# First feed-forward matrix by seven block products instead of eight

## The chip, the cores and the metric

The kernel runs on one core of a Trainium2 chip, as one launch. The metric is device time in microseconds, the median of several runs. TensorE multiplies matrices into PSUM banks, VectorE (DVE) and ScalarE (ACT) do elementwise work and read PSUM, GpSimd (POOL) does elementwise work in SBUF, and the DMA queues move data; SyncE's queue (SP) issues the loads of weights.

## The reference

One inference step of a two-layer encoder over 512 prompt positions and 32 positions of a later chunk, 544 columns together, in float32. Each of the two layers is

```
x = LN_0(alpha*x + 0.5*SwiGLU_1(x))           # d = 1024, hidden 2816
proj = x @ w_in                               # pooling, short convolution, q, k, v
x = LN_1(alpha*x + concat(pool, conv, attn) @ w_out)
x = LN_2(alpha*x + 0.5*SwiGLU_2(x))

def swiglu(x, w_in, w_out):
    gate, up = jnp.split(x @ w_in, 2, axis=-1)
    return (jax.nn.silu(gate) * up) @ w_out
```

so there are four feed-forward (SwiGLU) layers, each with a first matrix of 1024 x 5632 (gate and up) and a second of 2816 x 1024. The outputs are y, the new keys and values, and the states of pooling and convolution.

## The kernel before

Activations stand transposed: 8 tiles (k = 0 to 7) of 128 features by T = 544 columns, which are treated as two halves of HALF = 272 (`HS`), since a PSUM bank holds 512 floats. `y` is the residual in float32. The matmuls run on pairs of float32r tiles: `split` writes a rounded part (`hh`, by ScalarE) and the rest (`hl`, by VectorE). A product is three matmuls, high weights by high input and low weights by high input (`mm_h`, L199) and high weights by low input (`mm_l`, L204), summed in PSUM.

`Weights` streams the weights in the order of `specs`. `load` (L163) fetches one tile of 128 x 1024 (or 128 x 896) into a `raw` buffer, of which there are two, through SP's queue, and `group` splits it by 512 columns into `whi` (ScalarE, L159) and `wlo` (VectorE, L160); the ring has W_BUFS = 8 groups, and `get` keeps the loads two tiles ahead. All instructions pass through a framework that adds the semaphores and fixes, before the run, each engine's order of instructions; instructions written earlier have priority, but one whose buffer isn't free yet can be passed.

`ffn` goes over the 22 hidden tiles in three parts (FSPLIT = 8, 7, 7). A hidden tile is two weight tiles, gate and up: `mm2` runs 2 halves x 8 k x 3 matmuls for each; then ScalarE takes Silu of the gate (L448), VectorE multiplies by the up (L449), and `split` makes the pair `hx`. After each part the second matrix adds its contribution, 8 output tiles of 48 or 42 matmuls, into `y` (`resid`, L343 and L345). The last part is `out_phase`, which runs normalisation (`LN`) beside its last matmuls: sums of squares, `stats`, `spread`, then per k `centre` (L316) and `scale` (L322, L327, L332, and GpSimd's L333). The next stage's first two weight tiles are multiplied in `start`, half by half as the normalised tiles appear; their accumulators are handed on as `pre`. There are six PSUM banks in the pool `ps` and two in `po`.

Of the kernel before, what the change touches and what calls it, by code (L numbers as in the profile page):

```python
# [10 lines left out]
F32 = mybir.dt.float32  # L11
# [17 lines left out]
NF = D_FF // P  # L29
FSPLIT = (8, 7, 7)  # L30
NB = 2
W_BUFS = 8
RAW_BUFS = 2
# [15 lines left out]
UW = 640  # L49

# [17 lines left out]
def encoder_kernel(  # L68
# [28 lines left out]
    tp = ctx.enter_context(tc.tile_pool(name="tp", bufs=4))  # L97
# [46 lines left out]

    class Weights:


        def __init__(self, specs):
            self.specs, self.used, self.loaded, self.ready = specs, 0, 0, []

        def fetch(self):
            self.loaded += 1
            return wp.tile([P, NK * P], F32, tag="raw", name="raw", bufs=RAW_BUFS)

        def group(self, raw, g, n):
            e = min(G, n - g)
            hi = wp.tile([P, G], F32R, tag="whi", name="whi", bufs=W_BUFS)
            lo = wp.tile([P, G], F32R, tag="wlo", name="wlo", bufs=W_BUFS)
            S.activation(out=hi[:, :e], in_=raw[:, g:g + e], func=AF.Copy)  # L159
            V.tensor_tensor(out=lo[:, :e], in0=raw[:, g:g + e], in1=hi[:, :e].bitcast(F32), op=ALU.subtract)  # L160
            return hi, lo

        def load(self):  # L163
            src, n = self.specs[self.loaded]
            raw = self.fetch()
            nc.sync.dma_start(out=raw[:, :n], in_=src)
            self.ready.append([self.group(raw, g, n) for g in range(0, n, G)])

        def first(self, x):

            specs = self.specs[:2]
            raws = [self.fetch() for _ in specs]
            self.ready = [[], []]
            for i in range(NK // 4):
                ks, cs = slice(4 * i, 4 * i + 4), slice(i * G, (i + 1) * G)
                nc.sync.dma_start(out=ya[:, ks, HS[0]], in_=xT[:, ks, HS[0]])
                for (src, n), raw in zip(specs, raws):
                    nc.sync.dma_start(out=raw[:, cs], in_=src[:, cs])
                for k in range(NK)[ks]:
                    split(y[k], x[k], HS[0])  # L180
                for raw, out in zip(raws, self.ready):
                    out.append(self.group(raw, i * G, NK * P))
            nc.sync.dma_start(out=ya[:, :, HS[1]], in_=xT[:, :, HS[1]])

        def ahead(self, n):

            while self.loaded < min(self.used + n, len(self.specs)):
                self.load()

        def get(self, n=2):  # L190
            self.used += 1
            self.ahead(n)
            return self.ready.pop(0)

    def mm_h(acc, w, x, k, h, first):

        cs = slice((k % 4) * P, (k % 4) * P + P)
        for i, v in enumerate(w[k // 4]):
            PE.matmul(acc[:, :HALF], v[:, cs], x[k][0][:, HS[h]], start=first and i == 0, stop=False)  # L199

    def mm_l(acc, w, x, k, h, last):

        cs = slice((k % 4) * P, (k % 4) * P + P)
        PE.matmul(acc[:, :HALF], w[k // 4][0][:, cs], x[k][1][:, HS[h]], start=False, stop=last)  # L204
# [30 lines left out]

    class LN:
# [9 lines left out]
        def ln_tile(self, name):  # L246
            return tp.tile([P, T], F32, tag="ln", name=name, bufs=3)

        def half_tile(self, tag, name, bufs):
            return tp.tile([P, HALF], F32, tag=tag, name=name, bufs=bufs)  # L250
# [29 lines left out]
        def add_last(self, m, acc, h):  # L280
            c, q = y[m][:, HS[h]], self.half_tile("z", "sq", 4)
# [23 lines left out]
        def spread(self, h, psum):  # L305

            d = self.half_tile("dg", "diag", 2)[:CH].rearrange("p (c t) -> p c t", c=NCH)
# [10 lines left out]
        def scale(self, h, k):  # L318
            l, j, sl = self.l, self.j, HS[h]
            c = y[k][:, sl]  # L320
            z = self.half_tile("z", "z", 4)
# [25 lines left out]
    def out_phase(l, j, x, ks, alpha):  # L347
# [4 lines left out]
        first = NK - nb  # L352
        for m in range(first):
# [37 lines left out]
        if ln.final:  # L391
# [7 lines left out]
            mean = ln.half_tile("dg", "mean", 2)  # L399
# [13 lines left out]
    def start(x, step, hooks, done):  # L413

        ws = [W.get(0), W.get(0)]
        accs = [(bank(), bank()), (bank(), bank())]
        todo = [(h, k) for h in range(2) for k in range(NK)][done:]
        for h in range(2):
            for k in range(NK):
# [8 lines left out]
                if h == 1 and k in (3, 6):  # L428
                    W.ahead(k // 3)
# [4 lines left out]

    def ffn(l, f, x, pre):
        for s, n in enumerate(FSPLIT):
            hs = []
            for i in range(n):
                if pre:
                    ga, ua = pre  # L440
                    pre = None
# [542 lines left out]
```

## Time and profile before

| | us |
|---|---|
| median of 3 runs (lowest, highest) | 2107.07 (2106.86, 2107.29) |
| profiled execution, its own time | 2106.86 |
| its span, first to last instruction | 2104.7 |

| engine | busy us | share of the span | instructions |
|---|---|---|---|
| TensorE, matmuls | 2079.3 | 99% | 16286 |
| VectorE | 1013.1 | 48% | 1970 |
| ScalarE | 771.6 | 37% | 1591 |
| GpSimd | 228.8 | 11% | 216 |

The profile's page has the busy time of each engine, the span in 40 slices with a digit for the busy tenths, the chain of work that ended last followed back from the end, and the costliest groups of instructions: line, engine, operation, output and inputs, shape and count, then busy time and mean ns of one, then the engine's idle time just before them and what ended most of it. Matmuls are pipelined, so the time of one is longer than the distance from one to the next. The timeline merges neighbours of one kind into one row (x3 is three of them). HBM moved 179.88 MB in and 8.34 MB out.

### The profile page before, as it was taken

The numbers are of one execution on the slowest core, as the hardware profiler recorded it, in microseconds if no ns is written. First come the engines' busy times: TensorE is split into PE (matmuls) and PEld (weight loads), VectorE is DVE, ScalarE is ACT, GpSimd is POOL, SyncE is SP. The second block draws the span as 40 slices with busy tenths as digits, with TensorE's granted clock in tenths as the row PEclk, the third lists the DMA queues.
The fourth block names the chain that finished last, engine by engine and source line by source line (L and its number), as shares of the span: only waits on it lengthen the run. The fifth ranks groups of instructions, "written<-read, shape, count | busy, mean of one in ns | idle before, by whom it ended". The sixth has DMA issues, their size and how long they took to land.

```text
span 2104.7 us, 38545 instructions
## 1 busy us (share of the span) xinstructions
PE 2079.3 (99%) x16286; PEld 2042.2 (97%) x16286; DVE 1013.1 (48%) x1970; ACT 771.6 (37%) x1591; POOL 228.8 (11%) x216
## 2 busy tenths in 40 slices
PE   9999999999999999999999999999999999999997
PEld 9999999999999999999999999999999999999997
DVE  4333333776556333333653333347766553333337
ACT  5323223565435323223443232235653353222233
POOL 0000000511133000000420000006011320000003
PEclk9999999999999999999999999999999999999999
DMA  7322222132232222222232222222321222222221
GB/s 240 99 91 83 90 91 84 59 115 92 62 119 81 91 86 86 84 98 82 70 101 83 89 88 89 89 85 67 109 93 54 78 91 82 90 89 82 91 83 61
DMA packets 61749, 189.13 MB, mean 90 GB/s; under 512 B 8932, under 2 KB 13156, under 8 KB 61576
## 3 DMA queue, kind: packets, MB, share of 16 engines
q1 hardware_dynamic: 52592, 173.18, 25.9%
q10 hardware_dynamic: 8984, 13.49, 2.0%
q8 instruction: 128, 2.10, 0.4%
q14 instruction: 45, 0.37, 0.1%
HBM read 179.88 MB, written 8.34 MB: 89 GB/s over the span
## 4 chain that ended last, share of the span: by engine, by line
PE 95%; DVE 2%; POOL 1%; ACT 1%; issue 1%; DMA 0%; SPq 0%; POOLq 0%; ACTq 0%
PE b L199 59%; PE b L204 30%; PE b L629 1%; PE b L628 1%; PE o L644 1%; POOL xl L333 1%; PE b L609 0%; ACT ya L327 0%; DVE z L322 0%; PE b L716 0%; POOL rstd L302 0%; PE b L682 0%; DVE diag L308 0%; DVE acc L286 0%; PE b L311 0%
## 5 line engine op out<-in xcount | busy, mean ns | idle before, releaser
L199 PE MATMUL b<-xh,whi 128*128 128x272 f32 x3456 | 1000.0, 291 | 6.2 <-ACT xh L332 3.7
L199 PE MATMUL b<-xh,wlo 128*128 128x272 f32 x3456 | 993.5, 289 | 0.3 <-DVE wlo L160 0.3
L204 PE MATMUL b<-xl,whi 128*128 128x272 f32 x3456 | 978.2, 288 | 0.2
L160 DVE TENSOR_TENSOR wlo<-raw,whi 128x512 fp32r<-128x512 f32 (+1 forms) x656 | 469.7, 719 | 694.8 <-ACT whi L159 692.7
L159 ACT ACTIVATE whi<-raw 128x512 fp32r<-128x512 f32 (+1 forms) x656 | 403.3, 619 | 858.7 <-PE b L204 569.8
L199 PEld LDWEIGHTS b<-xh,whi 128*128 128x128 f32 x3456 | 651.7, 189 | 9.5 <-ACT xh L332 5.9
L199 PEld LDWEIGHTS b<-xh,wlo 128*128 128x128 f32 x3456 | 653.1, 189 | 1.5 <-DVE wlo L160 0.8
L204 PEld LDWEIGHTS b<-xl,whi 128*128 128x128 f32 x3456 | 644.6, 188 | 2.1 <-POOL xl L333 1.5
L199 PE MATMUL b<-hh,wlo 128*128 128x272 f32 x1408 | 406.2, 289 | 0.0
L199 PE MATMUL b<-hh,whi 128*128 128x272 f32 x1408 | 405.2, 288 | 0.0
L204 PE MATMUL b<-hl,whi 128*128 128x272 f32 x1408 | 404.6, 287 | 0.0
L199 PEld LDWEIGHTS b<-hh,wlo 128*128 128x128 f32 x1408 | 264.9, 188 | 0.2
L204 PEld LDWEIGHTS b<-hl,whi 128*128 128x128 f32 x1408 | 264.9, 188 | 0.2
L199 PEld LDWEIGHTS b<-hh,whi 128*128 128x128 f32 x1408 | 264.9, 188 | 0.0
L278 POOL TENSOR_TENSOR ya<-ya,shift 128x544 f32<-128x544 f32 x14 | 24.8, 1792 | 1412.9 <-DVE wlo L160 1386.4
L448 ACT ACTIVATE sg<-b 128x272 f32<-128x272 f32 x176 | 69.6, 397 | 213.1 <-PE b L204 213.0
L449 DVE SCALAR_TENSOR_TENSOR sg<-b,sg 128x272 f32<-128x272 f32 x176 | 77.6, 441 | 130.9 <-PE b L204 119.2
L343 DVE SCALAR_TENSOR_TENSOR ya<-ya,b 128x272 f32<-128x272 f32 x88 | 38.5, 438 | 88.7 <-PE b L204 87.8
L333 POOL TENSOR_TENSOR xl<-ya,xh 128x272 fp32r<-128x272 f32 x80 | 70.3, 901 | 30.8 <-ACT xh L332 25.1
L345 DVE TENSOR_TENSOR ya<-ya,b 128x272 f32<-128x272 f32 x108 | 46.7, 433 | 54.0 <-PE b L204 53.8
L232 ACT ACTIVATE hh<-sg 128x544 fp32r<-128x544 f32 (+1 forms) x100 | 59.1, 591 | 32.6 <-DVE sg L449 32.5
L233 DVE TENSOR_TENSOR hl<-sg,hh 128x544 fp32r<-128x544 f32 (+1 forms) x100 | 65.2, 652 | 7.2 <-ACT hh L232 7.1
(183 smaller groups left out, 1455.9 us busy)
## 6 DMA issues: line engine op xcount, KB each, us to landing
raw<-in_w SPq DMA_DIRECT2D x206, 512.0 KB, 3.5
raw<-in_w SPq DMA_DIRECT2D x64, 448.0 KB, 3.3
raw<-in_wi SPq DMA_DIRECT2D x40, 512.0 KB, 3.5
raw<-in_wo SPq DMA_DIRECT2D x16, 512.0 KB, 3.5
U<-scr ACTq DMA_DIRECT2D x8, 320.0 KB, 4.8
out_nkT<-k ACTq DMA_DIRECT2D x8, 272.0 KB, 2.1
out_nvT<-vT ACTq DMA_DIRECT2D x8, 272.0 KB, 2.1
out_yT<-ya SPq DMA_DIRECT2D x16, 136.0 KB, 1.8
```

What stands on the lines that cost most here:

```text
L159: S.activation(out=hi[:, :e], in_=raw[:, g:g + e], func=AF.Copy)
L160: V.tensor_tensor(out=lo[:, :e], in0=raw[:, g:g + e], in1=hi[:, :e].bitcast(F32), op=ALU.subtract)
L199: PE.matmul(acc[:, :HALF], v[:, cs], x[k][0][:, HS[h]], start=first and i == 0, stop=False)
L204: PE.matmul(acc[:, :HALF], w[k // 4][0][:, cs], x[k][1][:, HS[h]], start=False, stop=last)
L232: S.activation(out=hh[:, sl], in_=t[:, sl], func=AF.Copy)
L233: (eng or V).tensor_tensor(out=hl[:, sl], in0=t[:, sl], in1=hh[:, sl].bitcast(F32), op=ALU.subtract)
L278: POOL.tensor_tensor(out=c, in0=c, in1=self.s, op=ALU.subtract)
L333: POOL.tensor_tensor(out=xl[:, sl], in0=c, in1=xh[:, sl].bitcast(F32), op=ALU.subtract)
L343: V.scalar_tensor_tensor(out=c, in0=c, scalar=ALPHA, in1=a, op0=ALU.mult, op1=ALU.add)
L345: V.tensor_tensor(out=c, in0=c, in1=a, op=ALU.add)
L448: S.activation(out=sg[:, sl], in_=g[:, :HALF], func=AF.Silu)
L449: V.scalar_tensor_tensor(out=sg[:, sl], in0=u[:, :HALF], scalar=0.5, in1=sg[:, sl], op0=ALU.mult, op1=ALU.mult)
```

## The change

The first matrix of a hidden tile is a product of 2 x 2 blocks: rows gate and up (2 blocks of 128), the sum over k in two parts (k = 0 to 3 and 4 to 7), columns in two halves. Before, that is eight block products of four k each. Now 20 of the 22 hidden tiles of each feed-forward layer take seven (the Strassen-Winograd form), of sums of weight blocks with sums of input blocks; the first two (NPLAIN = 2) keep eight. The second matrix is unchanged.

- `Weights.sums`: a tile's four blocks of 128 x 512 (two fetches of 512 KB) give seven groups to be split instead of four, with four VectorE additions in float32. The ring is 10 groups instead of 8, `raw` 3 buffers instead of 2; loads run one such tile ahead (`get`).
- `Blocks`: once a feed-forward layer, for each of four pairs (k, k + 4) of the normalised input, four VectorE operations of 272 columns make the sums `s56` and `s73`, and two splits make the pairs that are multiplied.
- `seven`: the products, 12 matmuls each, into three banks in the order a, b, a, c, a, c, a. The products in a are summed up there, and so are those in c; after each product `after[i]` reads the bank (`hidden`): after 1, 3 and 4 a copy by ScalarE, after 2, 5, 6 and 7 an operation by VectorE. A product that adds to a bank must wait for the reading before it.
- `plan`: a part of the second matrix comes one hidden tile later than before, but for the last. The last hidden tile is split whole, not by halves.
- Memory: the normalisation's tiles and the block sums share a pool of XB = 18 tiles (`big`), whose place the mixer's tiles take in between, and `out_phase` of the mixer is called after the mixer's pool is closed. `tmp` has 5 buffers instead of 4.

```diff
 FSPLIT = (8, 7, 7)
+NPLAIN = 2
-W_BUFS = 8
-RAW_BUFS = 2
+W_BUFS = 10
+RAW_BUFS = 3
...
+XB = 18
...
+        def add(self, a, b):
+            r = big["pool"].tile([P, G], F32, tag="sum", name="sum", bufs=4)
+            V.tensor_tensor(out=r, in0=a, in1=b, op=ALU.add)
+            return r
+
+        def sums(self, src):
+            b11, b12, b22, b21 = self.blocks(src)
+            g11, g21 = self.group(b11), self.group(b21)
+            r1 = self.add(b11, b12)
+            r2 = self.add(r1, b22)
+            g2, g1 = self.group(r2), self.group(r1)
+            g3 = self.group(self.add(b12, b22))
+            g22 = self.group(b22)
+            return g11, g21, g2, g1, g3, g22, self.group(self.add(r2, b21))
...
-        def get(self, n=2):
+        def get(self, n=None):
+            if n is None:
+                n = 2 if self.units[self.used][0] == "t" else 1
             self.used += 1
             self.ahead(n)
             return self.ready.pop(0)
...
+    class Blocks:
+        def __init__(self, plain):
+            self.plain, self.sums = plain, []
+            for k in range(NK // 2):
+                self.add(y[k], y[k + NK // 2])
+
+        def add(self, e, o):
+            h0, h1 = HS
+            t1, t2 = tmp("s56"), tmp("s73")
+            V.tensor_tensor(out=t1[:, h0], in0=e[:, h1], in1=o[:, h1], op=ALU.subtract)
+            V.tensor_tensor(out=t1[:, h1], in0=t1[:, h0], in1=e[:, h0], op=ALU.subtract)
+            V.tensor_tensor(out=t2[:, h0], in0=e[:, h0], in1=e[:, h1], op=ALU.subtract)
+            V.tensor_tensor(out=t2[:, h1], in0=o[:, h0], in1=t1[:, h1], op=ALU.add)
+            s = [new_b(n) for n in ("s56", "s73")]
+            split(t1, s[0])
+            split(t2, s[1])
+            self.sums.append(s)
+
+        def products(self):
+            e, o = self.plain[:NK // 2], self.plain[NK // 2:]
+            s56, s73 = ([s[i] for s in self.sums] for i in range(2))
+            for xs, h in ((e, 0), (o, 0), (s56, 1), (s56, 0), (s73, 0), (s73, 1), (o, 1)):
+                yield [tuple(v[:, HS[h]] for v in x) for x in xs]
+
+    def seven(ws, blocks, after):
+        banks = {}
+        for i, (w, xs, name) in enumerate(zip(ws, blocks.products(), "abacaca")):
+            opens = name not in banks
+            acc = banks.setdefault(name, bank() if opens else None)
+            for j, (xh, xl) in enumerate(xs):
+                cs = slice(j * P, (j + 1) * P)
+                for m, (v, x) in enumerate(((w[0], xh), (w[1], xh), (w[0], xl))):
+                    PE.matmul(acc[:, :HALF], v[:, cs], x, start=opens and j == 0 and m == 0,
+                              stop=j == len(xs) - 1 and m == 2, skip_group_check=True)
+            after[i](acc[:, :HALF])
...
         def ln_tile(self, name):
-            return tp.tile([P, T], F32, tag="ln", name=name, bufs=3)
+            return big["pool"].tile([P, T], F32, tag="xb", name=name, bufs=XB)
...
+    def hidden(ws, blocks):
+        sg = tmp("sg")
+        up = tp.tile([P, HALF], F32, tag="up", name="up", bufs=2)
+        h0, h1 = HS
+        copy = lambda out: lambda acc: S.activation(out=out, in_=acc, func=AF.Copy)
+
+        def times(u, sl):
+            V.scalar_tensor_tensor(out=sg[:, sl], in0=u, scalar=0.5, in1=sg[:, sl], op0=ALU.mult, op1=ALU.mult)
+
+        def c12(acc):
+            V.tensor_tensor(out=sg[:, h0], in0=acc, in1=sg[:, h0], op=ALU.subtract)
+            S.activation(out=sg, in_=sg, func=AF.Silu)
+            times(up, h0)
+
+        seven(ws, blocks, [
+            copy(up),
+            lambda acc: V.tensor_tensor(out=up, in0=acc, in1=up, op=ALU.add),
+            copy(sg[:, h0]),
+            copy(sg[:, h1]),
+            lambda acc: V.tensor_tensor(out=sg[:, h1], in0=sg[:, h1], in1=acc, op=ALU.subtract),
+            c12,
+            lambda acc: times(acc, h1),
+        ])
+        return sg
+
+    def plan():
+        ends = [sum(FSPLIT[:s + 1]) for s in range(len(FSPLIT))]
+        for i in range(NF):
+            yield 1, i
+            if i in ends:
+                yield 2, ends.index(i)
+        yield 2, len(FSPLIT) - 1
+
     def ffn(l, f, x, pre):
+        xb = Blocks(x)
...
+                    sg = hidden(W.get(), xb)
+                hs.append(new_x("h"))
+                split(sg, hs[-1])
...
+            big["pool"] = tc.alloc_tile_pool(name="xb", bufs=1, reuse_waits="tile")
+        x, pre = ffn(l, 0, x, pre)
+        big["pool"].release()
+        with tc.tile_pool(name=f"at{l}", bufs=1, reuse_waits="tile") as ap:
+            mix = mixer(l, x, pre, ap)
+        big["pool"] = tc.alloc_tile_pool(name="xb", bufs=1, reuse_waits="tile")
+        x, pre = out_phase(l, 1, mix, (4, 5, 6, 0, 1, 2, 3, 7), True)
         x, pre = ffn(l, 1, x, pre)
+    big["pool"].release()
```

The host lays the first matrix out by blocks (`_blocks`).

More of the change, by code (lines that the diff above doesn't have):

```diff
@@ L161, in group, with blocks @@
             return hi, lo
-        def load(self):
[L164 to L167, printed above, removed]
+        def blocks(self, src):
+            out = []
+            for i in range(2):
+                raw = self.fetch()
+                nc.sync.dma_start(out=raw, in_=src[:, 2 * i * G:2 * (i + 1) * G])
+                out += [raw[:, :G], raw[:, G:]]
+            return out
@@ new lines, in load @@
+        def load(self):
+            kind, src, n = self.units[self.loaded]
+            self.loaded += 1
+            if kind == "t":
+                raw = self.fetch()
+                nc.sync.dma_start(out=raw[:, :n], in_=src)
+                out = Tile([self.group(raw[:, g:min(g + G, n)]) for g in range(0, n, G)])
+            elif kind == "p":
+                out = self.pair([self.group(b) for b in self.blocks(src)])
+            else:
+                out = self.sums(src)
+            self.ready.append(out)
@@ L169, in first @@
         def first(self, x):
-            specs = self.specs[:2]
-            raws = [self.fetch() for _ in specs]
-            self.ready = [[], []]
+            src, n = self.units[0][1], G
+            out = []
             for i in range(NK // 4):
-                ks, cs = slice(4 * i, 4 * i + 4), slice(i * G, (i + 1) * G)
+                ks = slice(4 * i, 4 * i + 4)
                 nc.sync.dma_start(out=ya[:, ks, HS[0]], in_=xT[:, ks, HS[0]])
-                for (src, n), raw in zip(specs, raws):
-                    nc.sync.dma_start(out=raw[:, cs], in_=src[:, cs])
+                raw = self.fetch()
+                for c in range(2):
+                    nc.sync.dma_start(out=raw[:, c * n:(c + 1) * n], in_=src[:, (2 * i + c) * n:(2 * i + c + 1) * n])
@@ L193, in get, with two @@
             return self.ready.pop(0)
+        def two(self):
+            return self.get(0) if self.units[self.used][0] == "p" else [self.get(0), self.get(0)]
     def mm_h(acc, w, x, k, h, first):
-        cs = slice((k % 4) * P, (k % 4) * P + P)
-        for i, v in enumerate(w[k // 4]):
-            PE.matmul(acc[:, :HALF], v[:, cs], x[k][0][:, HS[h]], start=first and i == 0, stop=False)
+        for i, v in enumerate(w.at(k)):
+            PE.matmul(acc[:, :HALF], v, x[k][0][:, HS[h]], start=first and i == 0, stop=False)
     def mm_l(acc, w, x, k, h, last):
-        cs = slice((k % 4) * P, (k % 4) * P + P)
-        PE.matmul(acc[:, :HALF], w[k // 4][0][:, cs], x[k][1][:, HS[h]], start=False, stop=last)
+        PE.matmul(acc[:, :HALF], w.at(k)[0], x[k][1][:, HS[h]], start=False, stop=last)
     def mm(acc, w, x, ks, h):
@@ L427, in start @@
                     f()
-                if h == 1 and k in (3, 6):
-                    W.ahead(k // 3)
+                if h == 1 and k == 3:
+                    W.ahead(1)
             for acc, w in zip(accs, ws):
@@ L917, in _fm, with _blocks @@
     return a.transpose(n - 1, *range(n - 3), n - 2, n - 3)
+def _blocks(a):
+    b = [a[:, :, :, c, :, r] for r, c in ((0, 0), (0, 1), (1, 1), (1, 0))]
+    b = np.stack(b, axis=4)
+    return b.reshape(*b.shape[:4], -1)
 def kernel(**inputs):
```

120 lines of the change are left out of this document (61 added, 59 removed).

## The prediction

> **What bounds the kernel now.** I read the page first: engine totals, slices, chain, costliest groups.
>
> ```profile
> span 2104.7 us, 38545 instructions
> PE 2079.3 (99%) x16286; PEld 2042.2 (97%) x16286; DVE 1013.1 (48%) x1970; ACT 771.6 (37%) x1591; POOL 228.8 (11%) x216
> PE   9999999999999999999999999999999999999997
> DVE  4333333776556333333653333347766553333337
> PE 95%; DVE 2%; POOL 1%; ACT 1%; issue 1%; DMA 0%; SPq 0%; POOLq 0%; ACTq 0%
> L199 PE MATMUL b<-xh,whi 128*128 128x272 f32 x3456 | 1000.0, 291 | 6.2 <-ACT xh L332 3.7
> ```
>
> TensorE is busy in every slice, carries 95% of the chain that ended last, and its commonest matmul waited 6.2 us in 1000. So the kernel takes as long as its matmuls do, and a matmul taken out is time saved, as long as nothing else rises to the same level. The 291 ns are not a matmul's price, since matmuls overlap; their rate comes from a busy stretch, here two hundred microseconds inside the first feed-forward layer (columns: stretch, length, then busy time and count by engine):
>
> ```profile
> 100.00:300.00 200.00, 200.00 (x1602) 200.00 (x1602) 74.03 (x130) 54.06 (x98) 0.00 (x0) 1.00 0.28 88
> ```
>
> 200.00 / 1602 = 0.1248 us per matmul at full clock. In the same stretch VectorE (third) worked 74 us and ScalarE (fourth) 54: this is the room into which the change puts its additions.
>
> The sum is made against the profiled execution, 2106.86 us (its span and 2.2 us around it), which is 0.2 us under the median of the runs, 2107.07.
>
> **1. Matmuls removed.** A hidden tile (gate and up, two halves, eight k, three matmuls each) takes 2 x 2 x 8 x 3 = 96 matmuls, 11.98 us. Seven products of four k take 7 x 4 x 3 = 84, 10.48 us; one product is 12, 1.50 us. Twenty of the 22 hidden tiles of each of the four feed-forward layers change: 80 x 12 x 0.1248 = **-119.8 us**. The second matrix and the mixer keep their matmuls.
>
> **2. VectorE and ScalarE in a seven-product tile.** The instructions concerned, all shapes kept apart:
>
> ```profile
> L160 DVE TENSOR_TENSOR wlo<-raw,whi 128x512 fp32r<-128x512 f32 x592 | 427.5, 726 | 677.1 <-ACT whi L159 675.0
> L159 ACT ACTIVATE whi<-raw 128x512 fp32r<-128x512 f32 x592 | 369.9, 630 | 829.3 <-PE b L204 540.4 <-issue 265.2 <-DMA raw<-in_w 15.7
> L449 DVE SCALAR_TENSOR_TENSOR sg<-b,sg 128x272 f32<-128x272 f32 x176 | 77.6, 441 | 130.9 <-PE b L204 119.2 <-ACT sg L448 3.9
> L448 ACT ACTIVATE sg<-b 128x272 f32<-128x272 f32 x176 | 69.6, 397 | 213.1 <-PE b L204 213.0
> L233 DVE TENSOR_TENSOR hl<-sg,hh 128x544 fp32r<-128x544 f32 x76 | 54.7, 720 | 1.2 <-ACT hh L232 1.1
> L232 ACT ACTIVATE hh<-sg 128x544 fp32r<-128x544 f32 x76 | 48.9, 643 | 0.8 <-DVE sg L449 0.7
> L160 DVE TENSOR_TENSOR wlo<-raw,whi x656: 557/693/1858, 6.5 to 2069.3; 128x512 fp32r<-128x512 f32 x164
> ```
>
> The last row has least, median and longest: the usual split takes 0.693 us; the mean of 726 comes from those beside GpSimd. Whether durations add up is seen in merged timeline rows (start, length, count at the end):
>
> ```profile
> 26.95 1.89 DVE L160 TENSOR_TENSOR wlo<-raw,whi 128x512 fp32r<-128x512 f32 x3
> 13.00 2.90 DVE L233 TENSOR_TENSOR xl<-ya,xh 128x272 fp32r<-128x272 f32 x8 [0.79 <-ACT xh L232]
> 26.18 2.18 ACT L159 ACTIVATE whi<-raw 128x512 fp32r<-128x512 f32 x4
> 102.55 0.44 DVE L449 SCALAR_TENSOR_TENSOR sg<-b,sg 128x272 f32<-128x272 f32 x1 [1.37 <-PE b L204]
> 103.02 0.43 ACT L232 ACTIVATE hh<-sg 128x272 fp32r<-128x272 f32 x1 [2.57 <-DVE sg L449]
> 1067.44 1.29 DVE L160 TENSOR_TENSOR wlo<-raw,whi 128x512 fp32r<-128x512 f32 x2
> ```
>
> Three in 1.89 us: the next begins (1.89 - 0.69) / 2 = 0.60 us after the one before, under its duration; for 272 elements (2.90 - 0.43) / 7 = 0.35; for ScalarE (2.18 - 0.63) / 3 = 0.52. (The last three rows are for the waits and the start below.)
>
> VectorE has after the change 7 splits and 4 additions of weight blocks (11 of 512 elements, where it had 4), 5 of 272 out of the products (it had 2), and one split of 544. At full durations: 11 x 0.693 + 5 x 0.441 + 0.720 = 10.55 us. Back to back: 11 x 0.60 + 5 x 0.35 + 0.64 (0.60 scaled) = 9.0 us. TensorE has 10.48. So VectorE comes to between 86% and 101% of TensorE: the change spends nearly all the room. ScalarE: 7 x 0.630 + 3 x 0.397 + 2 x 0.643 = 6.9 us, 66%. I take VectorE near the lower value, because an engine that falls behind has its inputs waiting and then runs back to back; TensorE stays the bound, and splits cost nothing as long as this holds.
>
> The Trainium skill, "VectorE: DVE Perf Modes", section "The DRAIN you can't avoid", has it that after every VectorE operation the pipe must empty before the next starts, which would make the sum by full durations the right one, and VectorE the bound by a hair. The rows disagree (0.60 against 0.693), and the page adds that a next operation that is not held starts earlier; so that sum is kept below as a rival.
>
> **The new waits** are in the banks. Products 1, 3, 5 and 7 add into one bank, 4 and 6 into another, and the running sum is read out between them. So product 3 waits for ScalarE's copy after 1, product 5 for the copy after 3, product 6 for the copy after 4, and product 7 for VectorE's subtraction after 5; one product, 1.50 us, lies between each time. A copy takes 0.397 and the subtraction 0.441; with one split in progress ahead (0.63 or 0.69) and 0.2 for the handing over (an estimate: a matmul ends 0.291 - 0.125 = 0.17 after the next could start, and ScalarE began 0.03 after VectorE's end at 102.99) it is 1.23 to 1.33 us: free. With two splits ahead it is 0.63 + 0.63 + 0.40 + 0.2 = 1.86: 0.36 us of TensorE, and every later matmul queues behind it. Bounds: 0, and 80 x 4 x 0.36 = 115. The loads of the next tile are written ahead of this tile's read-outs, but the ring lets only as many of them through as products have ended; I take 0.15 us a tile, **+12**.
>
> **3. Block sums of the input**, once a layer: 4 x (4 operations of 272 and 2 splits of 544) on VectorE, 16 x 0.35 + 8 x 0.64 = 10.7 to 16 x 0.441 + 8 x 0.720 = 12.8 us; 8 x 0.643 = 5.1 on ScalarE. They need both halves of the normalised input, so they come when normalisation ends; product 3 of the third hidden tile is the first to read them. The start of the third feed-forward layer, on VectorE and GpSimd:
>
> ```profile
> 1055.79 8.71 POOL L333 TENSOR_TENSOR xl<-ya,xh 128x272 fp32r<-128x272 f32 x9 [0.26 <-ACT xh L332]
> 1057.80 2.15 DVE L160 TENSOR_TENSOR wlo<-raw,whi 128x512 fp32r<-128x512 f32 x2
> 1060.57 0.77 DVE L322 TENSOR_TENSOR z<-ya,b 128x272 f32<-128x272 f32 x2
> 1061.27 1.86 DVE L160 TENSOR_TENSOR wlo<-raw,whi 128x512 fp32r<-128x512 f32 x2
> 1065.58 0.43 DVE L449 SCALAR_TENSOR_TENSOR sg<-b,sg 128x272 f32<-128x272 f32 x1
> 1056.00:1070.00 14.00, 13.86 (x109) 13.43 (x108) 11.55 (x22) 10.49 (x24) 8.36 (x9) 1.00 0.37 119
> 1064.80:1076.80 12.00, 12.00 (x97) 12.00 (x97) 6.17 (x11) 5.33 (x11) 0.00 (x0) 1.00 0.51 165
> 20.00:40.00 20.00, 20.00 (x154) 18.73 (x153) 7.32 (x18) 11.40 (x21) 0.31 (x1) 1.00 0.60 167
> ```
>
> Normalisation leaves VectorE at 1061.3; the first hidden tile's matmuls end near 1065 (its last read-out starts at 1065.58). The second, still plain, takes 12, two products 3.0: product 3 is due at 1080, 18.7 us after VectorE is free. Wanted until then: the block sums 11.8 (middle), read-outs and splits of two tiles 2.5, four weight splits left over (my count of the second tile's) at 0.93 (1.86 / 2, beside GpSimd) 3.7, and five operations for the first three weight groups 3.2: 21.2, some 2.5 us too much. VectorE then still owes the ring the next tile's groups, written ahead of the read-outs: at most 10 operations of 0.65, so 9 us in the worst order and 0 in the best. I take 4 at each of the three layers behind a normalisation. The first layer has VectorE free for 12.7 of its 20 us from 20.00 on, about the sums' price: 2. Together **+14**, bounds 0 and 32.
>
> By the Trainium skill, "SBUF — State Buffer", section "Who interferes with whom", a VectorE operation with two SBUF inputs contends with GpSimd operations that read SBUF. The trace agrees: the pairs of splits above take 1.86 and 2.15 us beside GpSimd against 1.29 at 1067.44. That is in the 0.93, and since GpSimd is idle from 1064.5 on, no more comes of it.
>
> **4. Edits with one answer.** The last hidden tile is split whole instead of by halves: 0.441 + 0.643 + 0.720 + signals, 2.0 us, under the 18 matmuls of the other six tiles that come first (2.25 us); 0, at most 1 us a layer. Weight bytes stay; a tile still takes two transfers of half a megabyte,
>
> ```profile
> raw<-in_w SPq DMA_DIRECT2D x206, 512.0 KB, 3.5
> U<-scr ACTq DMA_DIRECT2D x8, 320.0 KB, 4.8
> ```
>
> now 7.0 us of SP's queue in 10.48 with a third buffer: 0. The mixer's tiles lie where the normalisation's lay, so the bias rows U (second row), on ScalarE's queue, can't be fetched before it ends; they are wanted after the rest of the start and one projection, some 9 us later, and take 4.8: 0; uncovered, 5 a layer.
>
> **Sum:** 2106.9 - 119.8 + 12 + 14 = **2013 us**.
>
> **Rivals.** *VectorE becomes the bound.* If its instructions mostly don't overlap (10.55), and the chain block sum, ScalarE, VectorE leaves gaps of some 0.05 at its 16 instructions, a tile takes 11.3 us: 2106.9 - 80 x (11.98 - 11.3) + 14 = 2066. For it: the ranges nearly touch, and
>
> ```profile
> DVE wlo L160 <- ACT whi L159: 692.7, 493, 3.8
> ACT whi L159 <- PE b L204: 569.8, 384, 4.4
> ```
>
> 493 of 656 splits waited for ScalarE, so few ran back to back. Against it: these waits are of an idle engine ahead of its time, ended by buffers that TensorE frees.
>
> *Slower: the banks.* If each of the four read-outs stands behind two splits, 115 us go instead of 12: 2106.9 - 119.8 + 115 + 14 = 2116; if VectorE's stands behind three (0.693 x 3 + 0.441 + 0.2 - 1.50 = 1.22 us instead of 0.36), 2185. It decides from (119.8 - 14) / 320 = 0.33 us a read-out. For it: in program order the next tile's splits come first. Against it: the ring, and ScalarE's 66%.
>
> *All hidden:* neither term costs, 1987. That the product of twelve matmuls is slower per matmul than 0.1248 (more waits at its beginning) would be the change not doing what it says; across the tile boundaries in the stretch above the rate shows nothing of it.
>
> **How the numbers follow.** Forecast (1987 to 2035) 0.64; below it 0.04; VectorE the bound (2035 to 2100) 0.20; no change, 0.03; slower by the banks 0.09. Within 0.2%, 4 us, a measurement of this kernel can't tell. The range is 1987, all hidden, to 2075, beyond the VectorE case's centre: it leaves out 0.04 below and some 0.17 above. Faster 0.88, same 0.03, slower 0.09.
>
> **What would show it.** After: 960 matmuls fewer (15,326 in all); 0.125 us between matmuls inside a product; VectorE near 60% of the span and, inside the seven-product tiles, 85 to 95%; TensorE idle little ahead of products 3 to 7 (waits on ScalarE's copies and VectorE's subtraction, under 12 us), and 2 to 6 us around product 3 of the third hidden tile of layers 2 to 4. A span set by VectorE would show it busy all through those tiles with TensorE waiting for weight groups; the bank case would show waits on the copies hundreds of times, a few tenths each. Wrong would be a time over 2075, or one in which the seven-product tiles take their 10.48 us and the loss sits elsewhere.

## The result, and the profile after

| | us |
|---|---|
| before, median of 4 runs (lowest, highest) | 2106.97 (2105.69, 2107.29) |
| after, median of 4 runs (lowest, highest) | 2022.49 (2021.50, 2023.92) |
| ratio, 95% interval | 0.9601 [0.9584, 0.9617] |
| profiled span, granted clock: before | 2104.7, 0.994 |
| profiled span, granted clock: after | 2019.7, 0.985 |

The change gains 84.5 us, where the matmuls taken out are worth 119.8. The forecast was 2013, with a range of 1987 to 2075. The page of the changed kernel: span, engine totals, VectorE's slices, the chain by engine, and three groups of matmuls (count, then busy us and mean ns of one, then idle time before them and what ended it).

```profile
span 2019.7 us, 37955 instructions
PE 1974.7 (98%) x15326; PEld 1935.6 (96%) x15326; DVE 1476.5 (73%) x2854; ACT 1002.9 (50%) x2009; POOL 225.1 (11%) x216
DVE  7957767777658966858698586777766599577677
PE 89%; DVE 6%; ACT 2%; DMA 1%; issue 1%; POOL 1%; SPq 0%; ACTq 0%
L254 PE MATMUL b<-xh,whi 128*128 128x272 f32 x896 | 270.4, 306 | 24.8 <-ACT sg L591 12.2
L342 PE MATMUL b<-s56h,whi 128*128 128x272 f32 x640 | 184.5, 288 | 1.3 <-ACT up L552 1.3
L342 PE MATMUL b<-s73h,whi 128*128 128x272 f32 x640 | 184.6, 288 | 0.6 <-ACT sg L552 0.6
```

TensorE has 960 matmuls fewer and is still the bound, but its share of the chain fell from 95% to 89%. The matmuls of the new products (L342) wait hardly at all. Those that wait are the plain matmuls on the normalised input (L254, x896): 24.8 us, against 6.2 before.

Five seven-product tiles of the first layer, from the third product of one tile to that of the fifth tile behind it; then the first three of them alone; and below it a stretch at the third layer's normalisation (stretch, length, then busy time and count of TensorE's matmuls and weight loads, VectorE, ScalarE and GpSimd, then the granted clock):

```profile
58.30:110.86 52.56, 52.56 (x423) 52.56 (x421) 45.68 (x81) 32.46 (x60) 0.00 (x0) 1.00 0.32 100
58.32:89.84 31.52, 31.52 (x254) 31.52 (x253) 28.81 (x52) 19.47 (x36) 0.00 (x0) 1.00 0.31 101
1013.10:1019.90 6.80, 6.80 (x39) 6.80 (x39) 3.54 (x10) 3.92 (x11) 5.04 (x7) 0.50 0.00 1
```

A tile takes 52.56 / 5 = 10.51 us with TensorE busy throughout: the steady state is what the change promised. VectorE is 45.68 / 52.56 = 87% busy over the five, of which the last prepares weights of the second matrix, which need no additions; the three tiles of the second row, which have all their additions, take 28.81 / 3 = 9.6 us of VectorE each, 91%. The third row has the other side: here the record of the clock says half, and TensorE started a matmul every 6.80 / 39 = 0.174 us on the mean. From 1016.05 on it was every 0.23, but from 1014.0 to 1015.7 every 0.11, so the record covers more than the slow stretch.

What TensorE waited for in the changed kernel (what waited, for what; us in total, times, longest):

```profile
PE b L254 <- ACT sg L591: 12.2, 3, 8.1
PE b L254 <- ACT xh L443: 10.4, 5, 2.1
PE b L422 <- DVE diag L419: 4.0, 3, 2.9
PE b L342 <- ACT up L552: 1.3, 2, 0.8
PE b L342 <- ACT sg L552: 0.6, 2, 0.3
```

and in the kernel before:

```profile
PE b L311 <- DVE diag L308: 8.2, 6, 2.9
PE b L199 <- ACT xh L332: 3.7, 7, 1.0
```

Nearly the whole loss, 32 us of 35, can be counted from the starts of successive matmuls, each step taken over 0.125 us. Steps above 0.3 us (waits) add up to 57.2 us before and 77.1 after; steps of 0.20 to 0.26 (matmuls at half clock) to 21.8 and 34.0. So of the 119.8 some 20 us went into longer waits and 12 into time at half clock; in the records of the clock, half clock outside the last stretch of the span grew from 17.1 us to 51.2, in stretches of 3.4, 6.8 and 10.2 us.

By place (starts of matmuls against 0.1248 us each, the changed kernel less the kernel before), the first 60 us have 11.5 us of the loss, the starts of the second, third and fourth feed-forward layers 7.4, 5.7 and 6.8, and the two mixers 2.2 and 1.6; the stretches between have next to none.

**The first start.** The longest wait by far, 8.1 us, is in the first layer. Timeline of the changed kernel, rows of TensorE, ScalarE and VectorE:

```profile
27.89 0.29 PE L258 MATMUL b<-xl,whi 128*128 128x272 f32 x1
36.24 0.59 PE L254 MATMUL b<-xh,whi 128*128 128x272 f32 x1 [8.06 <-ACT sg L591]
36.63 0.43 PE L254 MATMUL b<-xh,wlo 128*128 128x272 f32 x1
36.86 0.43 PE L258 MATMUL b<-xl,whi 128*128 128x272 f32 x1
33.84 0.64 ACT L286 ACTIVATE s73h<-s 128x544 fp32r<-128x544 f32 x1
34.49 1.28 ACT L591 ACT_TABLE_LOAD   x1
35.79 0.40 ACT L591 ACTIVATE sg<-b 128x272 f32<-128x272 f32 x1
33.69 0.71 DVE L287 TENSOR_TENSOR s73l<-s,s73h 128x544 fp32r<-128x544 f32 x1
```

The second hidden tile's matmuls need a PSUM bank that the first tile still holds, until its Silu (L591) reads it at 35.79. That Silu stands in ScalarE's order behind six of the eight splits of the block sums (L286): `Blocks` is written ahead of it. The eight temporaries of `Blocks` come out of the same five buffers as Silu's output `sg`, the ninth, so `sg` may also have waited for a buffer that the VectorE row sets free, at 33.69 + 0.71 = 34.40. The row ACT_TABLE_LOAD just ahead of Silu takes 1.28 us of the wait. When TensorE resumes, its matmuls come 0.23 us apart. The same wait is seen twice more, 2.08 us at 655.86 and 2.06 at 1652.95.

**The normalisation.** The third layer's start in the changed kernel, GpSimd, VectorE and TensorE:

```profile
1005.32 1.01 POOL L413 TENSOR_TENSOR rstd<-var,mhalf 68x4 f32<-68x4 f32 x1 [4.92 <-DVE var L412]
1006.28 0.69 DVE L175 TENSOR_TENSOR wlo<-raw,whi 128x512 fp32r<-128x512 f32 x1 [0.71 <-ACT whi L174]
1008.45 0.43 DVE L419 TENSOR_TENSOR diag<-ident,rstd 68x272 f32<-68x272 f32 x1
1008.94 0.72 PE L422 MATMUL b<-diag,ones 68*128 68x272 f32 x2 [0.79 <-DVE diag L419]
1011.72 0.40 PE L254 MATMUL b<-xh,whi 128*128 128x272 f32 x1 [2.06 <-ACT xh L443]
```

and in the kernel before:

```profile
1042.73 1.01 POOL L302 TENSOR_TENSOR rstd<-var,mhalf 68x4 f32<-68x4 f32 x1 [4.44 <-DVE var L301]
1043.78 0.44 DVE L308 TENSOR_TENSOR diag<-ident,rstd 68x272 f32<-68x272 f32 x1 [0.24 <-POOL rstd L302]
1047.35 0.39 PE L199 MATMUL b<-xh,whi 128*128 128x272 f32 x1 [0.98 <-ACT xh L332]
```

Before, `diag` began 0.04 us after its input `rstd` was done (1042.73 + 1.01 = 1043.74). After, it began 2.12 us after it (1008.45 against 1006.33), because VectorE's order had a weight split ahead of it that waited for ScalarE, and then additions of the last output tile. Some 1.4 us after the wait of 2.06 the clock halved, for 6.8 us (the windows row above).

### The profile page after: what moved, and what is told of

Read it like the earlier page. It is cut to its first block, busy times and chain, and to the rows that moved or that the text cites. A ratio compares the mean times of both kernels' runs of the same rounds, so it can differ in the third digit from the quotient of the medians.

```text
span 2019.7 us, 37955 instructions
## 1 busy us (share of the span) xinstructions
PE 1974.7 (98%) x15326; PEld 1935.6 (96%) x15326; DVE 1476.5 (73%) x2854; ACT 1002.9 (50%) x2009; POOL 225.1 (11%) x216
## 4 chain that ended last, share of the span: by engine, by line
PE 89%; DVE 6%; ACT 2%; DMA 1%; issue 1%; POOL 1%; SPq 0%; ACTq 0%
PE b L342 41%; PE b L254 28%; PE b L258 14%; DMA raw<-in_w 1%; PE b L773 1%; PE b L772 1%; DVE wlo L175 1%; PE o L788 1%; DVE z L433 1%; POOL xl L444 1%; ACT ya L438 1%; ACT whi L174 1%; DVE sum L206 1%; DVE ya L427 1%; PE b L753 0%
## 5 line engine op out<-in xcount | busy, mean ns | idle before, releaser
L174 ACT ACTIVATE whi<-raw 128x512 fp32r<-128x512 f32 x576 | 353.8, 618 | 510.8 <-PE b L258 304.6
L175 DVE TENSOR_TENSOR wlo<-raw,whi 128x512 fp32r<-128x512 f32 x576 | 403.2, 703 | 165.6 <-ACT whi L174 161.7
L254 PE MATMUL b<-hh,whi 128*128 128x272 f32 x1408 | 405.7, 288 | 0.0
L254 PE MATMUL b<-hh,wlo 128*128 128x272 f32 x1408 | 405.5, 288 | 0.0
L174 ACT ACTIVATE whi<-sum 128x512 fp32r<-128x512 f32 x320 | 200.9, 631 | 210.8 <-PE b L258 100.0
L254 PE MATMUL b<-xh,whi 128*128 128x272 f32 x896 | 270.4, 306 | 24.8 <-ACT sg L591 12.2
L175 DVE TENSOR_TENSOR wlo<-sum,whi 128x512 fp32r<-128x512 f32 x320 | 218.7, 688 | 87.4 <-ACT whi L174 79.9
L342 PE MATMUL b<-xh,wlo 128*128 128x272 f32 x960 | 276.2, 288 | 0.0
L342 PE MATMUL b<-xh,whi 128*128 128x272 f32 x960 | 276.1, 288 | 0.0
L342 PE MATMUL b<-xl,whi 128*128 128x272 f32 x960 | 275.2, 287 | 0.0
L254 PEld LDWEIGHTS b<-hh,whi 128*128 128x128 f32 x1408 | 265.0, 188 | 0.1
L254 PEld LDWEIGHTS b<-hh,wlo 128*128 128x128 f32 x1408 | 264.9, 188 | 0.1
L254 PE MATMUL b<-xh,wlo 128*128 128x272 f32 x896 | 261.7, 296 | 0.3 <-DVE wlo L175 0.3
L258 PE MATMUL b<-xl,whi 128*128 128x272 f32 x896 | 248.1, 297 | 1.4 <-POOL xl L444 1.4
L254 PEld LDWEIGHTS b<-xh,whi 128*128 128x128 f32 x896 | 175.1, 196 | 30.5 <-ACT xh L443 13.5
L342 PE MATMUL b<-s56h,whi 128*128 128x272 f32 x640 | 184.5, 288 | 1.3 <-ACT up L552 1.3
L342 PE MATMUL b<-s73h,whi 128*128 128x272 f32 x640 | 184.6, 288 | 0.6 <-ACT sg L552 0.6
L342 PE MATMUL b<-s56h,wlo 128*128 128x272 f32 x640 | 184.5, 289 | 0.0
L342 PE MATMUL b<-s73h,wlo 128*128 128x272 f32 x640 | 183.9, 287 | 0.0
L342 PE MATMUL b<-s73l,whi 128*128 128x272 f32 x640 | 183.9, 287 | 0.0
```

The lines of the kernel that those rows point to most:

```text
L174: S.activation(out=hi[:, :n], in_=raw, func=AF.Copy)
L175: V.tensor_tensor(out=lo[:, :n], in0=raw, in1=hi[:, :n].bitcast(F32), op=ALU.subtract)
L254: PE.matmul(acc[:, :HALF], v, x[k][0][:, HS[h]], start=first and i == 0, stop=False)
L258: PE.matmul(acc[:, :HALF], w.at(k)[0], x[k][1][:, HS[h]], start=False, stop=last)
L342: PE.matmul(acc[:, :HALF], v[:, cs], x, start=opens and j == 0 and m == 0, stop=j == len(xs) - 1 and m == 2, skip_group_check=True)
```

## The experiments

Each is the changed kernel with one edit, unless an earlier experiment is named as its base, and is timed against the kernel before (medians of 2107.16 to 2107.94 beside them). The first four runs tell the seven products from the other edits, and the places of the loss from each other; the next asked whether VectorE and the ring are near their limits; the rest went after the normalisation.

**Everything but the seven products** (e1_plain).

```diff
-NPLAIN = 2
+NPLAIN = 22
-        xb = Blocks(x)
+        xb = None
```

> All 22 hidden tiles by eight products (no block sums of weights or input), every other edit kept: ring of 10, third raw buffer, order of the second matrix, shared pool. Theory (what the change brings is the 960 matmuls, what it loses is lost where a stage starts): 16286 matmuls again, the feed-forward starts without block sums about as before, the starts of the mixer 5 us worse each as in the trace of after: 2107 + 10 = 2117 us, 2105 to 2122. Rival (the other edits are free, the whole loss of 35 us comes from the block sums): 2107 us within 3.

2117.77 us (2116.58 to 2118.14), ratio 1.0046 [1.0031, 1.0061]. TensorE's waits, and a matmul of the timeline at the kernel's start:

```profile
PE b L254 <- ACT xh L443: 10.6, 6, 2.1
PE b L422 <- DVE diag L419: 7.0, 5, 2.9
```

```profile
8.95 0.59 PE L254 MATMUL b<-xh,whi 128*128 128x272 f32 x1 [0.86 <-ACT whi L174]
```

So the other edits cost 10.6 us by themselves, with the waits for `xh` at the normalisation all there, and the seven products are worth 2117.8 - 2022.5 = 95.3 us. Counted by place as above, the first 60 us lose 3.1 us (a wait for the first weights, last row, and matmuls 0.23 us apart behind it), the starts of layers 2 to 4 0.6, 3.8 and 0.3, the mixers 2.3 and 1.8. The mixers thus lose without the seven products what they lose with them, and what the block sums add lies at the feed-forward starts.

**Block sums after the first tile** (e2_early).

```diff
-        xb = Blocks(x)
         hs = []
...
                 split(sg, hs[-1])
+                if i == 0:
+                    xb = Blocks(x)
                 continue
```

> The block sums of the input are written after the first hidden tile's Silu, product and split instead of before them. Theory (TensorE's waits of 8.35, 2.36 and 2.35 us at the second hidden tile are for banks that the first tile's late Silu holds): these go, with the half clock behind the first, 8.2 + 2.2 + 2.2 + 3.4 = 16 us, of which 2 to 4 come back at product 3 of the third tile: 2009 us, 2004 to 2014. Rival (VectorE simply has too much to do there, the wait moves on to the block sums' first reader): 2019 to 2024.

2010.42 us (2009.85 to 2010.88), ratio 0.9538 [0.9523, 0.9552]: 12.1 us faster than the changed kernel, as expected, and the fastest of all that was run. Its waits and its first Silu on ScalarE (both halves in one row):

```profile
PE b L254 <- ACT xh L443: 10.6, 6, 2.1
PE b L422 <- DVE diag L419: 7.1, 5, 2.9
PE b L342 <- ACT sg L590: 2.0, 1, 2.0
```

```profile
23.49 0.69 ACT L590 ACTIVATE sg<-b 128x272 f32<-128x272 f32 x2
```

Silu comes at 23.49 instead of 35.79, and of the 12.2 us of waits for it 2.0 are left, now one tile later. The stretch from 20 to 46 us, here and then in the changed kernel and in the one before:

```profile
20.00:46.00 26.00, 23.29 (x163) 21.58 (x162) 22.19 (x47) 17.81 (x33) 0.00 (x0) 0.93 0.44 131
```

```profile
20.00:46.00 26.00, 17.94 (x120) 16.45 (x119) 23.77 (x51) 14.59 (x28) 0.00 (x0) 0.87 0.48 136
```

```profile
20.00:46.00 26.00, 26.00 (x202) 24.73 (x201) 10.21 (x22) 14.17 (x26) 0.31 (x1) 1.00 0.64 186
```

The changed kernel starts 82 matmuls fewer in it than the kernel before, 82 x 0.1248 = 10.2 us; with the sums moved it is 39 fewer, 4.9 us. Silu's late turn is shown as the cause; whether it came late by its place in the order alone or by the ring of five temporaries was not told apart.

**Idle time at the normalisation filled with matmuls** (e3_fill): three more `spread` matmuls into a bank that nothing reads.

```diff
             PE.matmul(b[:, :HALF], ones[:CH, :], d.rearrange("p c t -> p (c t)"), start=True, stop=True)
+            if h == 0:
+                junk = side()
+                for _ in range(FILL):
+                    PE.matmul(junk[:, :HALF], ones[:CH, :], d.rearrange("p c t -> p (c t)"), start=True, stop=True)
```

> Three idle repeats of the spreading matmul into a free bank at each normalisation (six stages, about 0.7 us each), behind the real one, where TensorE waits 2 us for the first normalised tile; nothing else changed. Theory (the wait itself is short, what costs is the half clock of 6.8 us that follows it, 3.4 us a time): the clock stays full at the five starts behind a normalisation, 5 x 3.4 = 17 us less, about 0.3 us of overshoot a time: 2007 us, 2003 to 2013. Rival (the half clock does not come from that wait, or the repeats delay the real work): 2021 to 2028.

2025.94 us (2022.88 to 2028.56), ratio 0.9614 [0.9595, 0.9634]: a miss, no gain. Two stretches of it:

```profile
31.70:41.90 10.20, 4.76 (x21) 4.76 (x22) 10.20 (x21) 7.92 (x14) 0.00 (x0) 0.50 0.37 87
1013.10:1019.90 6.80, 6.12 (x53) 5.72 (x52) 4.99 (x14) 5.12 (x14) 5.97 (x8) 1.00 0.00 1
```

At 1013.10 the half clock is gone (1.00, 53 matmuls instead of 39), but others got longer (10.2 us at 31.7 instead of 6.8 at 33.4) or are new; together it is 47.8 us instead of 51.2. At this place the half clock went with the wait, which fits the theory that it comes from the wait; at other normalisations it stayed (6.8 us at 396.9 and at 1393.6), and the sum gained nothing.

**Products 2 and 3 swapped** (e7_adjacent), so that the reading of the first bank has nothing between.

```diff
+        todo = list(enumerate(zip(ws, blocks.products(), "abacaca")))
+        todo[1], todo[2] = todo[2], todo[1]
-        for i, (w, xs, name) in enumerate(zip(ws, blocks.products(), "abacaca")):
+        for i, (w, xs, name) in todo:
```

> Products 2 and 3 change places, so the product that adds to the first bank follows the one before it directly, and TensorE stands through the whole reading of the bank once a tile. Theory (a reading costs 0.17 + 0.03 + 0.40 + signals, 0.6 to 0.8 us, and is hidden only by the product in between): 80 x 0.7 = 56 us more, 2078 us, 2065 to 2095; with one weight split ahead on ScalarE's queue 1.2 us, up to 2118. Rival (readings of a bank cost TensorE nothing): 2022 us.

2040.68 us (2039.45 to 2040.95), ratio 0.968 [0.9666, 0.9695]: 18.2 us slower, 0.23 us a tile, and less than expected. In the trace matmuls of the other product were ordered between, so the run bounds the price of an uncovered reading from below only. It does show that the order a, b, a, c, a, c, a hides something that isn't free.

**Weight additions doubled**, two of the four (e4_two, 160 VectorE instructions more) and all four (e4_four, 320 more; its edit is shown).

```diff
         def add(self, a, b):
             r = big["pool"].tile([P, G], F32, tag="sum", name="sum", bufs=4)
-            V.tensor_tensor(out=r, in0=a, in1=b, op=ALU.add)
+            for _ in range(2):
+                V.tensor_tensor(out=r, in0=a, in1=b, op=ALU.add)
             return r
```

> Two of the four weight additions of a seven-product tile are done twice (same result), 160 VectorE instructions of 512 elements more. Theory (VectorE's instructions overlap when it is pressed, 9.0 us of the tile's 10.48, so 1.4 us are free): 9.0 + 2 x 0.69 (a repeat waits for the one before it, so its whole duration counts) = 10.4 us, still under TensorE: 2022 us, up to 2032 with what it adds at the starts. Rival (full durations count, VectorE stands at 10.55 now): 11.9 us a tile, 80 x 1.4 = 115 more, 2137 us.

2022.33 us (2019.95 to 2022.90), ratio 0.9596 [0.9581, 0.961]: no difference from the changed kernel. Three full tiles of it:

```profile
60.80:92.59 31.79, 31.79 (x254) 31.67 (x253) 31.59 (x59) 19.36 (x36) 0.00 (x0) 1.00 0.31 106
```

VectorE is already 31.59 / 31.79 = 99% busy in them, and a tile still takes 10.6 us. By full durations its 19 instructions would need 10.55 + 2 x 0.69 = 11.9 us.

> All four weight additions of a seven-product tile done twice, 320 VectorE instructions more. Theory: 9.0 + 4 x 0.69 = 11.8 us a tile against 10.48 of TensorE: VectorE is now the bound, 80 x 1.3 = 104 more less what the parts of the second matrix take up: 2085 to 2130 us. Rival (full durations): 13.3 us, 80 x 2.8 = 225 more, 2247 us. A time within 10 us of 2022 would say that even less of VectorE is used than the theory has it.

2037.70 us (2036.21 to 2041.57), ratio 0.9673 [0.9657, 0.969]: 15.2 us more, far under what either theory gave. The same five tiles, a row of VectorE's timeline, and a wait that the changed kernel had not:

```profile
58.30:110.86 52.56, 52.54 (x420) 52.30 (x418) 52.29 (x96) 28.92 (x57) 0.00 (x0) 1.00 0.26 84
```

```profile
109.45 1.90 DVE L175 TENSOR_TENSOR wlo<-sum,whi 128x512 fp32r<-128x512 f32 x3
```

```profile
PE b L343 <- DVE wlo L175: 2.4, 10, 0.3
```

Three splits in 1.90 us are again 0.60 us apart, though each takes 0.69. VectorE is now 52.29 / 52.56 = 99% busy in these tiles and TensorE only begins to wait for weight groups. What VectorE falls behind by is probably taken up by the ring and the next part of the second matrix, which needs VectorE less; this was not tested. So the changed kernel has room for about two more additions a tile, and instructions of VectorE cost their distance of 0.60 us, not their duration.

**Ring of 8 groups in the changed kernel** (e6_ring8: `W_BUFS = 8`).

> The ring has 8 groups as before the change, the rest is the changed kernel. Theory (weights are ready many products ahead, TensorE waited for them 2 us in all): 2022 us, within 5. Rival (the ring of 10 is what keeps the next tile's splits from standing ahead of this tile's read-outs): some 0.3 us a tile, 2046 us or more.

2027.99 us (2025.63 to 2031.02), ratio 0.9629 [0.9613, 0.9645]. This is just outside the theory's 5 us and far from the rival's 2046. The two groups more are worth some 5 us, at the edge of what the intervals separate, and the gain does not hang on them.

**The first normalised half earlier in the order**: `spread` written before two parts of the last output tile, on top of e2_early (e8_spread); with the loads of the second plain tile put off as well (e9_defer); and put off alone (e12_late).

```diff
         ln.centre(0, 1)
+        ln.spread(0, bank)
         run(g)
...
-        ln.spread(0, bank)
```

```diff
-        tail = [W.get() for _ in range(nb)]
+        tail = [W.get() for _ in range(nb - 1)]
+        nxt = W.units[W.used + 1][0] if W.used + 1 < len(W.units) else "t"
+        tail.append(W.get(1 if nxt == "p" else 2))
```

> The early Silu as before (2010 us by itself), and the normalisation's chain freed: the spreading of the deviations is written one step earlier, ahead of the read-out that VectorE did before it, and the second plain tile's weights are loaded in the start instead of ahead of it. Theory (the rest of the loss is TensorE's longer wait at the normalisations, 10.6 us on the first normalised tile against 3.7 before, and the half clock behind it): waits 8 us less, half clock from 18.8 us lost to some 10: 1994 us, 1987 to 2003. Rivals: only the waits count, 2003 us; the deferred weights come late and TensorE waits for them instead, over 2010.

2012.71 us (2011.89 to 2014.24), ratio 0.9553 [0.9539, 0.9567]: a miss.

> As e2_early (2010.4 us), with the spread of the first half's factor written two parts of the last output tile earlier, so that diag and its matmuls come earlier in the order; weights are fetched as in the changed kernel (e9_defer changed that too and came to 2012.7). If the waits at the normalisation come from the order in which spread is written: the wait for xh falls from 10.6 to 5 us and the time to 2000 to 2006. If an earlier place only turns the wait for xh into one for diag, as in e9_defer: 2009 to 2014.

2018.96 us (2017.94 to 2021.62), ratio 0.958 [0.9563, 0.9597]: also a miss, slower than e2_early by 8.5. Its waits:

```profile
PE b L422 <- DVE diag L419: 17.8, 12, 2.9
PE b L254 <- ACT xh L443: 3.2, 2, 1.6
```

> As e2_early (2010.4 us), with the loads of the second plain hidden tile left until the start of the feed-forward layer, so that four weight groups fewer stand ahead of the normalisation's VectorE work. Between e8_spread (2019.0) and e9_defer (2012.7) this deferral was the only difference and was worth 6.3 us. Theory (the early fetch of a second pair is what makes diag and xh late): 2002 to 2006 us, the waits for xh and diag together under 13 us where e2_early has 17.7. Rival (any shift of the fixed order moves the waits and the half-clock windows about, with no gain of its own): 2008 to 2016, the sum of the two waits within 3 us of 17.7.

2014.67 us (2013.46 to 2015.17, 5 runs), ratio 0.9558 [0.9545, 0.9571]. Its waits:

```profile
PE b L254 <- ACT xh L443: 10.9, 10, 2.1
PE b L258 <- POOL xl L444: 9.6, 10, 2.9
PE b L422 <- DVE diag L419: 7.6, 6, 2.6
```

Putting off the loads was worth 6.3 us beside the earlier `spread` (2019.0 to 2012.7) and cost 4.3 without it (2010.4 to 2014.7). With `spread` earlier the wait goes from `xh` to `diag`; with the loads later it goes to GpSimd's `xl`, although this kernel had as little half clock as the one before the change, 17.1 us outside the last stretch. What the rival foretold came (the waits for `xh` and `diag` add up to 18.5 us, 2014.67 us in all): no one instruction was found that is late, and each shift of the order gave the wait to the next link of the same chain.

**Which of the other edits costs the 10.6 us of e1_plain?** On the base of e1_plain, first its ring, `raw` and `tmp` put back (e10_ring: 8, 2 and 4 buffers), then the normalisation's tiles back in buffers of their own as well (e11_lntiles).

```diff
         def ln_tile(self, name):
-            return big["pool"].tile([P, T], F32, tag="xb", name=name, bufs=XB)
+            return tp.tile([P, T], F32, tag="ln", name=name, bufs=3)
-        def half_tile(self, name):
-            return big["pool"].tile([P, T], F32, tag="xb", name=name, bufs=XB)[:, :HALF]
+        def half_tile(self, name):
+            tag, n = ("dg", 2) if name in ("diag", "mean") else ("z", 4)
+            return tp.tile([P, HALF], F32, tag=tag, name=name, bufs=n)
```

> All 22 hidden tiles plain (no seven products, no block sums), as in e1_plain, and the ring back to 8 groups, raw to 2 buffers, tmp to 4 as before the change. e1_plain was 10.6 us over the kernel before, with about 27 us at half clock and diag (L419) late behind a weight split that waited for ScalarE. Theory A (the deeper ring lets more weight splits stand ahead of diag in VectorE's order): most of the 10.6 goes, 2108 to 2111 us. Theory B (it is the order in which the framework places the normalisation's tiles, now in the shared pool of 18): no change, 2116 to 2119 us.

2133.17 us (2130.16 to 2135.51), ratio 1.0117 [1.0099, 1.0135]: 15.4 us slower than e1_plain. Theory A is wrong in sign: the additional buffers help, of the ring, of `raw` or of `tmp`, which were not told apart.

> As e10_ring, and the normalisation's tiles (ln, z, sq, diag, mean) back in their own buffers (3, 4 and 2) as before the change. Theory B: 2107 to 2110 us, where e10_ring stays near 2118. Theory A: equal to e10_ring within 2 us. If both stay near 2118, the cause is in what is left of the edits: the first two weight tiles fetched as one pair, the second matrix's parts a tile later, the last tile split whole, or the mixer's pool closed first.

2119.20 us (2118.06 to 2121.26), ratio 1.0052 [1.0037, 1.0068]. The normalisation's own buffers win back 14.0 us of e10_ring, so with the small ring the shared pool costs that much; what it costs with the large one was not run. The traces show what the pool does: before the change the first half's `diag` began 0.03 to 0.04 us after `rstd` at all six normalisations, in the changed kernel 0.75 to 2.12 us after it, in e1_plain and e10_ring 0.75 to 2.00, always behind two additions of the last output tile (L396, L397). In e11_lntiles it is 0.03 again at five of the six, and 1.40 at the third layer.

Yet with the buffers and the pool both put back the kernel is where e1_plain was, 11.3 us over the kernel before. So what is left costs as much by itself: the first two weight tiles fetched as a pair, the second matrix's parts a tile later, the last tile split whole, or the mixer's pool closed first. Two edits that the list above doesn't name belong to it too: the plain tiles multiply the up before the gate, and the start of a stage asks for its next loads once instead of twice. These were not tried one by one, and it stays open which it is.

## Why the prediction was right, and where not

- **Matmuls removed, -119.8:** right. 15,326 matmuls, and 52.56 / (5 x 84) = 0.1251 us for one in the seven-product tiles.
- **Read-outs of the banks, +12:** too much. The waits on the copies are 1.3 + 0.6 us, and none is listed for VectorE's subtractions. The reason given for a low value holds more fully than was taken: the ring lets one weight split through for each product that ends, so two splits hardly ever queue ahead of a read-out (read from the trace, not tested by itself).
- **VectorE and ScalarE in a tile:** right. VectorE took 9.6 us in a full tile, where 9.0 (back to back) to 10.55 was forecast, and 91% lies in the forecast 85 to 95%; ScalarE 32.46 / 5 = 6.5, against 6.9. The doubled additions confirm the 0.60, and the rival in which VectorE is the bound (2066) falls: at 99% busy it costs nothing with 160 additions more and 15 us with 320. The rule of full durations, which the prediction took from the Trainium skill ("VectorE: DVE Perf Modes", "The DRAIN you can't avoid") and kept as a rival, is not borne out. For the whole span 60% was a slip: the prediction's own terms, 80 tiles with 9.0 to 10.55 us where there were 4.4 before, add 370 to 490 us and the sums 47, which is 71 to 77%; it is 73%.
- **Block sums at the starts, +14:** the step that failed, in size and place. Of the 119.8 - 84.5 = 35.3 us that did not come, 1.9 are at the banks and 10.6 in the other edits, so some 23 remain for the starts. The count by place agrees: the four starts lose 11.5 + 7.4 + 5.7 + 6.8 = 31.4 us, of which e1_plain has 3.1 + 0.6 + 3.8 + 0.3 = 7.8. e2_early shows 12.1 of them to be the wait for the first tile's Silu and what hangs on it; some 11 are not assigned to a cause. The prediction counted VectorE's work up to product 3 of the third tile. What was late was ScalarE's read-out of the first tile, and it held up the second tile, behind the same block sums. TensorE's idle time of 2 to 6 us, forecast around product 3 of the third tile of layers 2 to 4, is only 0.3, 0.8 and 0.3 us there; the waits of 2.08 and 2.06 us, in layers 2 and 4, are at the second tile. Nor did the sums come behind GpSimd's work, as the prediction had it: at each of these three layers four of their 16 operations of 272 columns ran beside it and took 1.00 to 1.02 us instead of 0.43. The first layer, priced at 2 us because VectorE was free there, lost the most; why it lost more than the others was not tested.
- **Edits with one answer, 0:** wrong as a whole. They cost 10.6 us (e1_plain), some 3 at the kernel's start and much of the rest around the normalisations, which the prediction did not look at because no instruction was added there. There they changed what stands ahead of `diag` in an order that is fixed before the run: the additions of the last output tile, and at some of them weight splits.
- **The clock:** left out. Every term was reckoned at full clock, and some 12 us of the 35 went at half clock.
- **2013 against 2022.5:** the banks were priced 10 too high, the starts 9 and the edits 10.6 too low; together that is the difference of 9.5. That the total came out within 10 us is therefore in part luck: errors of opposite sign. One of the prediction's own signs of being wrong is met in part: the seven-product tiles take their 10.5 us, and more of the loss than forecast sits elsewhere.

## What to carry to other kernels

When a change takes work from the engine that bounds the kernel, the steady state is easy to forecast from distances between instructions (not their durations); the loss sits at the starts of stages, so follow there every buffer that the bounding engine needs back, and on every engine's order, to what has been written ahead of it. Work that "isn't needed yet" should be written after the read-outs that free a bank: moving one statement was worth 12 us here. An edit of rings, pools or the order of loads that adds no instruction can still move the order around a chain of short dependent steps; measure such edits alone, and don't expect that moving one link earlier shortens the chain.

## What the runs showed of the hardware

In the changed kernel TensorE's clock also halved behind waits of 0.79 and 2.06 us, for 6.8 us by the record, in part of which matmuls start 0.23 us apart instead of 0.125. In this kernel and the one before, all these stretches but the last of the span are 3.4, 6.8 or 10.2 us long, and their starts lie whole multiples of 3.413 us apart (33.444 and 391.844 us: 105 of them). Two such steps of 3.41 us in the changed kernel, TensorE's busy time first:

```profile
1009.66:1013.07 3.41, 1.35 (x10) 1.25 (x10) 3.37 (x10) 2.87 (x8) 1.20 (x2) 1.00 0.08 30
1651.36:1654.77 3.41, 1.82 (x14) 1.82 (x15) 3.41 (x9) 3.40 (x6) 0.00 (x0) 1.00 0.09 32
```

The first stands just before the half clock at 1013.1; in the steps just before the other half-clock stretches behind a wait TensorE was busy 0 to 1.36 us. The second holds most of the wait of 2.06 us that ends at 1652.95, and no half clock follows it. So in this kernel it mattered how a wait fell on these steps, and not its length alone. No threshold comes out of it: in e8_spread half clock followed a step with 2.58 us busy, and the two stretches in the mixers of the changed kernel (531.8 and 1531.9), which the kernel before has too, follow steps that were busy throughout.

The Trainium skill, "TensorE: Matmul & The Clock Gate", Part 1, gives a free-running window of 3413 ns and half clock after an idle one; the lengths and the distances agree with the window, and so does the first stretch, which begins inside the wait of 8.1 us behind a step without any matmul; but the other waits before half clock were below 3.4 us, so that its rule to avoid idle gaps above that is not enough in this kernel.
